# A hybrid decoder block: when block 0's attention is released, and how far apart the two parts of the gates lie

## The chip, the cores and the metric

One core of a Trainium2 chip runs the whole program. The metric is the device time of one execution in microseconds (us), the median of several runs. Engines: TensorE (PE) multiplies, VectorE (DVE), ScalarE (ACT) and GpSimd (POOL) do the elementwise work, SyncE (SP) and ACT issue the loads and stores.

## The reference

One layer, batch 1, 2048 tokens, width 1024, all in float32. The parts that matter here:

```python
h = modulate(rms_norm(x, g_pre_mix), shift_m, scale_m)
q_a, k_a, v_a, q_m, k_m, v_m, o_m, i_m, f_m, g_a, g_m = split(h @ w_in)
y_a = sliding_window_attention(rope(q_a), rope(k_a), v_a, sinks)    # window 128, 8 query heads, 2 kv heads of 64
y_m = sigmoid(o_m) * head_layer_norm(mlstm_chunkwise(silu(conv(q_m, k_m)), v_m, i_m, f_m))
mix = (sigmoid(g_a) * (y_a @ w_branch_attn) + sigmoid(g_m) * (y_m @ w_branch_mlstm)) @ w_out
x = x + gate_m * rms_norm(mix, g_post_mix)
h2 = modulate(rms_norm(x, g_pre_ffn), shift_f, scale_f)
x = x + gate_f * rms_norm((silu(h2 @ w_ffn_gate) * (h2 @ w_ffn_up)) @ w_ffn_down, g_post_ffn)
```

The attention of 128 query tokens is a softmax over the 256 keys of its own and the previous block of 128, with a learned sink per head. The mLSTM needs, per token and head, running sums of log f and a running maximum of the input gate: these come from `i_m` and `f_m`, and are "the gates" below.

## The kernel before, in words

The 2048 tokens are two superblocks (`sb`) of two token blocks `b0` and `b1` of 512. For every superblock PE computes, in this order: the q products of a block (512 columns), its key, value and gate products together (`kv`, 264 columns), and the mLSTM value products (`vm`), for b0 and then for b1; then the pairs (`om`, `qk`, `ga`, `gm`), each of which shares products between the two blocks; then mLSTM, branch projections and outputs. Matmuls are exact to about float32: each operand is split into a high and a low part in fp32r, and `mm3` (L212 is the line in `mm` that issues) multiplies high by high, high by low and low by high. The split of weights is `split`: a cast on ACT, a subtraction on DVE (L264 and L265, L267 and L268 where a load is split in two). Superblock 1 reads split weights of `kv`, `q` and `vm` that superblock 0 stored to DRAM (`w_kv_d`, `w_q_d`, `w_vm_d`, loads at L328 and L333).

**What sets the order.** `superblock` is a generator of `Part`s (some weights with the products that use them) and of small functions that are called where they stand. Beside it run streams: generators that are started with `spawn(gen, delay)` and yield, after each step, the delay until their next step. The delays (`L_...`, in ns) are counted in PE's planned time (`now`, to which each `mm` adds); `tick` issues whatever is due, and `finish` drives streams to their end. Last, the framework's scheduler reorders each engine's instructions by its own estimate of time, so a moved call shifts instructions on all engines around it.

**The streams of this change.** `gates(b)` has three steps. The first does elementwise work on the gates' 32 columns; after `L_GATE` the second transposes them (PE L217 on `gt`), scans them on DVE (L905, L909) and forms maxima (L910 to L918); after `L_SCAN` the third transposes the results (four 68-column transposes, PE L217 on `tm`) and copies them out.

`attention_stream(u)`, u = 0 or 1, does every second of the superblock's eight attention blocks of 128 queries: it loads the queries, keys and values (`at`, L954; written to `at_d` before), and `attention` does 24 score products (12 for block 0 of all), in two halves: after each, ACT copies the scores of the own keys (L985), and DVE puts in those of the window before (L987). Then the maxima (DVE L993 to L996), eight exponentials with their sums (ACT L1002), reciprocals (DVE L1003, L1004) and the division (POOL L1005). After `L_SOFT` PE transposes each half (L217 on `tm`), ACT (L1014) and DVE (L1018) copy the two masks of it, and PE multiplies with the values (16 products); ACT and DVE split the result (L1030, L1035), and ACT stores it. The two streams start `L_ATT2` apart. A stream waits at blocks of b1 until `ready` says that b1's q and kv exist.

`attend(b)` finishes the rotary work on q and k, sets `ready`, starts the two attention streams if b is b0, and starts `gates(b)`. In superblock 0 it is called for b0 behind b0's vm; in superblock 1 behind b0's kv, ahead of vm; for b1 behind a quarter of b1's vm. Scores, transposes and value products use four PSUM banks in turn (`mix`); projections use the others (`acc`), which ACT empties (for vm, L870).

Of the kernel before, what the change touches and what calls it, by code (L numbers as in the profile page):

```python
# [37 lines left out]

L_X, L_HT, L_HS = 16000.0, 1400.0, 1500.0
L_ROPE, L_ROPEK, L_QK, L_ATT2 = 5000.0, 2100.0, 1500.0, 3500.0  # L40
L_GATE, L_SCAN = 1800.0, 5500.0
L_SOFT, L_PT, L_PV = 8000.0, 1300.0, 1000.0
L_ML, L_KW, L_OUT, L_STATE = 3200.0, 2600.0, 1500.0, 1500.0
L_S, L_LN = 1800.0, 5000.0
# [29 lines left out]
def decoder_block(ctx: ExitStack, tc: tile.TileContext, a: dict, out: bass.AP, dbg=None):  # L74
# [49 lines left out]
    def tx(shape, dtype=F32):  # L124
        return tpool.tile(shape, dtype, tag="tx", name=nm("tx"), bufs=9)
# [93 lines left out]
    def spawn(gen, delay=0.0):  # L219
        st = [now[0] + delay, gen, False]  # L220
        streams.append(st)
        return st
# [15 lines left out]
    def finish(sts):  # L238
        for st in sts:
            while not st[2]:  # L240
                now[0] = max(now[0], min(q[0] for q in streams))
                tick()
# [190 lines left out]
    b1 = const.tile([P, 48], F32, name="b1")  # L433
# [130 lines left out]
    def hsums(names):  # L564

        for name in names:
            raw = HR.pop(name)
            lo = hc_part(name, 1)
            nc.sync.dma_start(lo.bitcast(F32), raw)
        yield L_HD  # L570
        for name in names:
            hi, lo = (hc_part(name, i) for i in range(2))
            for k in range(4):
                v = lo[:, k, :].bitcast(F32)
                A.copy(hi[:, k, :], v)
                V.tensor_tensor(lo[:, k, :], v, hi[:, k, :].bitcast(F32), op=ALU.subtract)
                yield L_HS
# [191 lines left out]
    def superblock(sb):  # L769
        b0, b1 = 2 * sb, 2 * sb + 1  # L770
# [8 lines left out]
        def rope(raw, heads, b, t):  # L779
            sin, cos = tables[sb]  # L780
            t += (b % 2) * NT
            W = heads * HD
            raw = raw[:, :W]
            src = raw.rearrange("p (h u f) -> p h u f", u=2, f=32)
            cb = cos[:, t, :].unsqueeze(1).to_broadcast([P, heads * 2, 32])
            sb_ = sin[:, t, :].unsqueeze(1).unsqueeze(1).to_broadcast([P, heads, 2, 32])
            z = tx([P, 512])
            zz = z[:, :W].rearrange("p (h u f) -> p h u f", u=2, f=32)
            rr = raw.rearrange("p (h f) -> p h f", f=32)
            V.tensor_tensor(zz, src[:, :, ::-1, :], sb_, op=ALU.mult)  # L790
            V.tensor_tensor(rr, rr, cb, op=ALU.mult)
            V.tensor_tensor(src[:, :, 0, :], src[:, :, 0, :], zz[:, :, 0, :], op=ALU.subtract)
            V.tensor_tensor(src[:, :, 1, :], src[:, :, 1, :], zz[:, :, 1, :], op=ALU.add)
            return raw, z

        def q_stream(b, t, yz):
            yield L_ROPE
            y, z = yz
            pt = mix_tile()
            for j in range(GQ):  # L800
                transpose(pt[:, j * P:(j + 1) * P], y[:, j * P:(j + 1) * P])
            hi, lo = z.bitcast(F32R), y.bitcast(F32R)
            A.activation(hi, pt, AF.Copy, scale=HD ** -0.5)
            V.scalar_tensor_tensor(lo, pt, HD ** -0.5, hi.bitcast(F32), op0=ALU.mult, op1=ALU.subtract)
            for i, q in enumerate((hi, lo)):
                nc.sync.dma_start(at_d[b * NT + t][:, i * 512:(i + 1) * 512], q.bitcast(F32))
# [50 lines left out]
        def q_kv(b):  # L857
            if b > 1:
                q = token_group(kept_weights("q"), KD, 512, lhs_h(b), evac_q(b), kept=True)
            else:  # L860
                q = token_group(srcs_rows(w_in, KD, C_Q), KD, 512, lhs_h(b), evac_q(b), pair_heads=True, store="q" if b else None)
            if b > 1:
                return q, token_group(kept_weights("kv"), KD, 264, lhs_h(b), evac_kv(b), kept=True)
            raw_kv = Raw(load_kv)
            return q, token_group([(raw_kv, (lambda r, j=j: r[:, j:j + 2, :]), j, 2) for j in range(0, KD, 2)], KD, 264, lhs_h(b), evac_kv(b), store="kv" if b else None)

        def vm(b):
            def evac(t, ps):
                v = tx([P, 512])
                A.copy(v, ps)  # L870
                nc.sync.dma_start(vm_d[b][:, t, :], v)
            if b > 1:
                yield from token_group(kept_weights("vm"), KD, 512, lhs_h(b), evac, kept=True)
            else:
                yield from token_group(srcs_rows(w_in, KD, C_VM), KD, 512, lhs_h(b), evac, store="vm" if b else None)
# [69 lines left out]
        def load_at(n, queue):  # L945
            a_ = at()
            af = a_.bitcast(F32)
            if n == 0:
                queue.dma_start(af[:, :AT_K], at_d[n][:, :AT_K])
                for c0, k in ((AT_K, 2), (AT_V, 1)):  # L950
                    v_, d_ = (z[:, c0:c0 + 2 * k * P].rearrange("p (i u k) -> p i u k", i=k, u=2)[:, :, 1, :] for z in (af, at_d[n]))
                    queue.dma_start(v_, d_)
            else:
                queue.dma_start(af, at_d[n])  # L954
            return a_
# [86 lines left out]
        def attention_stream(u):  # L1042
            a_ = None
            for i in range(u, 2 * NT, 2):
                n = b0 * NT + i
                if a_ is None:
                    while i >= ready[0]:
                        yield 1000.0
                    a_ = load_at(n, nc.sync)
                    yield L_LOAD  # L1050
                    a_ = yield from attention(n, a_, lambda: i + 2 < ready[0])
                else:
                    yield L_LOAD - 1500.0
                    a_ = yield from attention(n, a_, lambda: i + 2 < ready[0])
                done_att[0] += 1
                yield 500.0
# [3 lines left out]
        def attend(b):  # L1060
            finish(R["qk"])
            ready[0] = (b - b0 + 1) * NT
            if b == b0:
                R["att"] = [spawn(attention_stream(0), L_QK), spawn(attention_stream(1), L_QK + L_ATT2)]
            R["gs", b] = [spawn(gates(b), L_QK)]

        def end_attention(n):
# [285 lines left out]
        if sb == 0:  # L1353
            raws, rotated = {}, {}

            def late_q(t):
                yield from q_stream(b0, t, rope(raws[t], HQ, b0, t))

            def q_raw(t, ps):
                raws[t] = tx([P, 512])  # L1360
                A.copy(raws[t], ps)
                if t > 1:
                    R["qk"].append(spawn(late_q(t), L_KV0 + L_LATE * (t - 1)))

            def q_rope(t):
                rotated[t] = rope(raws[t], HQ, b0, t)

            def q_rest(t):
                for _ in q_stream(b0, t, rotated[t]):
                    pass  # L1370

            first.update(kv=kv0, evac=q_raw, rope=q_rope, rest=q_rest)
        else:
            yield start
            yield from q0
            yield from kv0
            yield lambda: attend(b0)
        yield from vm(b0)
        yield lambda: finish([hps[b1]])
        if sb == 0:  # L1380
            yield lambda: attend(b0)
        yield lambda: hps.update(t=spawn(hsums(("T2", "T4"))))
        q1, kv1 = (list(z) for z in q_kv(b1))
        yield from kv1
        yield from q1
        vm1 = list(vm(b1))
        yield from vm1[:len(vm1) // 4]
        yield lambda: attend(b1)
        yield from vm1[len(vm1) // 4:]

        def start_f():
# [809 lines left out]
    def program():  # L2201
        items = [it for sb in range(NSB) for it in superblock(sb)]
        last = max(i for i, it in enumerate(items) if isinstance(it, Part))
        first_block()
        yield from items[:last]
        yield lambda: next(phase2)
        yield from items[last:]
# [47 lines left out]
```

## Time and profile before

| | before |
|---|---|
| median of 3 runs | 2666.65 us (2666.62 to 2668.6) |
| profiled execution | 2664.19 us |
| its span, 36035 instructions | 2662.2 us |
| mean granted PE clock | 0.996 |
| PE busy | 2614.5 us (98%), 12546 products and transposes |
| DVE, ACT, POOL busy | 1935.3, 1281.4, 133.1 us |

A row of the profile names the engine, the line of the kernel, the operation, and output <- input with the names in the program; behind it stand sizes, counts and times. In rows of the timeline the two numbers ahead are start and duration in us, and a bracket shows idle time ahead of the row and what ended it. Products overlap on PE, so a row's duration is longer than the distance to the next.

### The profile page before, as it was taken

How to read it: one execution, taken by the hardware profiler on the slowest of the kernel's cores; microseconds unless marked ns; L12 is line 12 of the kernel's file. 1: busy time of each engine (PE TensorE's matmuls, PEld its weight loads, DVE VectorE, ACT ScalarE, POOL GpSimd, SP SyncE). 2: the span in 40 equal slices, each digit the busy share in tenths (PEclk: the TensorE clock that was granted, in tenths of full speed). 3: DMA queues.
4: the chain of work that ended last, by engine and by line, in shares of the span. 5: the costliest groups of instructions: out<-in, count | busy, mean ns of one | idle time of the engine just before them, and what ended most of it. 6: DMA issues, size and time to landing. Idle time of an engine off the chain costs nothing.

```text
span 2662.2 us, 36035 instructions
## 1 busy us (share of the span) xinstructions
PE 2614.5 (98%) x12546; PEld 2142.4 (80%) x12546; DVE 1935.3 (73%) x3758; ACT 1281.4 (48%) x2531; POOL 133.1 (5%) x181
## 2 busy tenths in 40 slices
PE   8999999999989999999999999999999999999998
PEld 6777788888877788888878888888778888888786
DVE  6878887768675988875877777776776767676466
ACT  6656544545654654454643433345544333333444
POOL 0000001101100000110000000000000000000000
PEclk9999999999999999999999999999999999999999
DMA  7794466897797545597766554547675323234556
GB/s 270 255 327 141 135 194 186 266 327 247 263 311 241 179 135 185 181 301 261 224 235 199 172 174 155 165 136 232 211 241 173 111 99 113 94 111 138 191 204 221
DMA packets 352166, 532.95 MB, mean 200 GB/s; under 512 B 23136, under 2 KB 209628, under 8 KB 345200
## 3 DMA queue, kind: packets, MB, share of 16 engines
q1 hardware_dynamic: 333768, 514.86, 57.8%
q10 hardware_dynamic: 18216, 15.79, 1.9%
q8 instruction: 99, 1.62, 0.2%
q14 instruction: 83, 0.68, 0.1%
HBM read 367.61 MB, written 154.57 MB: 196 GB/s over the span
## 4 chain that ended last, share of the span: by engine, by line
PE 88%; DVE 5%; DMA 4%; ACT 2%; issue 1%; POOL 0%; ACTq 0%; SPq 0%; DVEq 0%; POOLq 0%
PE acc L212 61%; PE mix L212 23%; PE mix L217 2%; DVE hl L1745 1%; PE acc L90 1%; PE mix L90 1%; ACT hl L1744 1%; DMA raw<-as_d 1%; ACT tm L1002 1%; DMA raw<-ws_d 0%; DMA raw<-w_kv_d 0%; DMA big<-in_x_dram 0%; DMA raw<-in_w_ffn_down_dram 0%; DMA at_d<-tx 0%; DMA raw<-in_w_in_dram 0%
## 5 line engine op out<-in xcount | busy, mean ns | idle before, releaser
L212 PE MATMUL acc<-big,hl 128*128 128x512 f32 x3936 | 936.0, 392 | 4.0 <-ACT hl L1744 1.8
L212 PEld LDWEIGHTS acc<-big,hl 128*128 128x128 f32 x3936 | 732.3, 188 | 164.4 <-issue 5.1
L1744 ACT CAST hl<-raw 128x512 fp32r<-128x512 f32 x732 | 439.9, 621 | 491.7 <-PE acc L212 216.3
L1745 DVE TENSOR_TENSOR hl<-raw,hl 128x512 fp32r<-128x512 f32 x732 | 496.6, 695 | 200.7 <-ACT hl L1744 197.1
L212 PE MATMUL acc<-whi,big 128*128 128x512 f32 (+1 forms) x896 | 279.3, 387 | 0.1
L212 PE MATMUL mix<-big,hl 128*128 128x512 f32 x1056 | 263.0, 390 | 1.8 <-ACT hl L1744 1.1
L212 PE MATMUL acc<-hl,hl 128*128 128x512 f32 x1008 | 237.3, 393 | 5.8 <-DVE hl L1745 3.0
L212 PEld LDWEIGHTS mix<-big,hl 128*128 128x128 f32 x1056 | 197.7, 188 | 44.6 <-ACT hl L1744 2.0
L212 PEld LDWEIGHTS acc<-hl,hl 128*128 128x128 f32 x1008 | 187.0, 188 | 51.5 <-DVE hl L1745 8.7
L212 PEld LDWEIGHTS acc<-whi,big 128*128 128x128 f32 x896 | 167.2, 189 | 33.3 <-ACT whi L264 0.4
L212 PE MATMUL mix<-hl,hl 128*128 128x512 f32 x792 | 182.6, 391 | 2.6 <-ACT hl L1744 1.8
L212 PEld LDWEIGHTS mix<-hl,hl 128*128 128x128 f32 x792 | 147.9, 188 | 36.5 <-ACT hl L1744 3.0
L212 PE MATMUL acc<-wlo,big 128*128 128x512 f32 (+1 forms) x448 | 173.4, 388 | 1.1 <-DVE wlo L265 1.1
L212 PE MATMUL acc<-big,whi 128*128 128x512 f32 x512 | 157.4, 393 | 0.0
L268 DVE TENSOR_TENSOR wlo<-raw,whi 128x1024 fp32r<-128x1024 f32 (+1 forms) x76 | 91.2, 1200 | 60.9 <-ACT whi L267 55.7
L267 ACT CAST whi<-raw 128x1024 fp32r<-128x1024 f32 (+1 forms) x76 | 78.3, 1031 | 93.9 <-PE acc L212 87.3
L492 POOL TENSOR_TENSOR rs<-ms,halves 128x1 f32<-128x1 f32 (+1 forms) x56 | 41.0, 739 | 1635.8 <-DVE ms L490 1589.2
L212 PE MATMUL mix<-hcT4h,hl 128*128 128x512 f32 x352 | 115.6, 389 | 0.7 <-ACT hl L1744 0.7
L212 PE MATMUL acc<-hcT2h,hl 128*128 128x512 f32 x352 | 115.5, 389 | 0.0
L212 PEld LDWEIGHTS acc<-big,whi 128*128 128x128 f32 x512 | 95.3, 188 | 19.3
L212 PEld LDWEIGHTS acc<-wlo,big 128*128 128x128 f32 x448 | 85.0, 190 | 18.8 <-DVE wlo L265 1.4
L212 PE MATMUL acc<-big,wlo 128*128 128x512 f32 x256 | 97.5, 392 | 0.0
(379 smaller groups left out, 3640.7 us busy)
## 6 DMA issues: line engine op xcount, KB each, us to landing
as_d<-w SPq DMA_DIRECT2D x154, 256.0 KB, 2.0
raw<-in_w_in_dram SPq DMA_DIRECT2D x36, 1024.0 KB, 5.4
raw<-as_d SPq DMA_DIRECT2D x70, 512.0 KB, 3.8
raw<-in_w_ffn_gate_dram SPq DMA_DIRECT2D x22, 1024.0 KB, 5.6
raw<-in_w_ffn_up_dram SPq DMA_DIRECT2D x22, 1024.0 KB, 6.0
raw<-ws_d SPq DMA_DIRECT2D x40, 512.0 KB, 4.7
tx<-in_w_ada_dram SPq DMA_DIRECT2D x64, 256.0 KB, 5.3
g_d<-tx SPq DMA_DIRECT2D x64, 256.0 KB, 4.5
```

The costliest lines, as they stand in the source:

```text
L90: self.last = tc.keep_in_program_order(f(*p, **k)).ins
L212: T.matmul(o, lhsT=lhsT, rhs=rhs, start=start, stop=stop, skip_group_check=resumed)
L217: T.transpose(o, i, ident[:k, :k])
L267: A.copy(hv, src)
L268: V.tensor_tensor(lv, src, hv.bitcast(F32), op=ALU.subtract)
L492: G.tensor_tensor(r[:, :n], ms[:, :n], nhalf[:, :n], op=ALU.pow)
L1002: A.activation(sc[jj][:, i, :], sc[jj][:, i, :], AF.Exp, bias=nm_[:, c:c + 1], accum_out=sums[:, c:c + 1])
L1744: A.copy(v(hi), src)
L1745: V.tensor_tensor(v(lo), src, v(hi).bitcast(F32), op=ALU.subtract)
```

## The change

`attend(b)` no longer starts the gates; a new `gate(b)` does, with the same delay. For b0, `gate(b0)` stands where `attend(b0)` stood, and `attend(b0)` stands behind the key and value products of b1, ahead of b1's q products in the program. For b1 both are called where `attend(b1)` was. `L_SCAN` goes from 5500 to 20000 ns of PE's planned time.

```diff
-L_GATE, L_SCAN = 1800.0, 5500.0
+L_GATE, L_SCAN = 1800.0, 20000.0
...
             if b == b0:
                 R["att"] = [spawn(attention_stream(0), L_QK), spawn(attention_stream(1), L_QK + L_ATT2)]
+
+        def gate(b):
             R["gs", b] = [spawn(gates(b), L_QK)]
...
             yield from q0
             yield from kv0
-            yield lambda: attend(b0)
+            yield lambda: gate(b0)
         yield from vm(b0)
         yield lambda: finish([hps[b1]])
         if sb == 0:
-            yield lambda: attend(b0)
+            yield lambda: gate(b0)
         yield lambda: hps.update(t=spawn(hsums(("T2", "T4"))))
         q1, kv1 = (list(z) for z in q_kv(b1))
         yield from kv1
+        yield lambda: attend(b0)
         yield from q1
         vm1 = list(vm(b1))
         yield from vm1[:len(vm1) // 4]
-        yield lambda: attend(b1)
+        yield lambda: (attend(b1), gate(b1))
         yield from vm1[len(vm1) // 4:]
```

No instruction is added or taken away, and lines behind the new function stand two or three lower. PE's order is the same up to the second half of b1's kv in superblock 0, differs from there to some way into the pairs, where the attention ends, and differs again over the like stretch of superblock 1.

PE before, superblock 0, at the second half of b1's kv (`whi`, `wlo` are the split weights, `acc` the bank of the kv products, `mix<-at` scores, `tm_1222` the gates' rows):

```order
L212 MATMUL acc_1142<-whi_1193,big_767 128x264
L212 MATMUL acc_1143<-whi_1193,big_767 128x264
L217 MATMUL mix_1339<-ident,tm_1222 128x68 x4
L212 MATMUL mix_1366<-at_1247 128x256 x6
L212 MATMUL mix_1367<-at_1247 128x256 x6
L212 MATMUL mix_1384<-at_1247 128x256 x6
L212 MATMUL acc_1140<-wlo_1194,big_767 128x264
```

PE of the change, the same place:

```order
L212 MATMUL acc_1143<-wlo_1135,big_678 128x264
L212 MATMUL acc_1143<-whi_1134,big_679 128x264
L212 MATMUL acc_1140<-whi_1189,big_767 128x264
L212 MATMUL acc_1141<-whi_1189,big_767 128x264
L212 MATMUL acc_1142<-whi_1189,big_767 128x264
L212 MATMUL acc_1143<-whi_1189,big_767 128x264
L212 MATMUL acc_1140<-wlo_1190,big_767 128x264
```

Scores and gate transposes no longer stand between the products with the high part of the weights and the first one with the low part.

PE of the change, superblock 0, where b1's vm ends and the first pair begins (`at_1667` and `at_1714` are two attention blocks, `tm_1722` and `tm_1723` the two halves of the first one's softmax, `tm_1822` of the second's, `tx` rows of rotary work, `acc_2539` the pair's first bank):

```order
L212 MATMUL mix_1842<-at_1714 128x256
L212 MATMUL mix_1843<-at_1714 128x256
L217 MATMUL mix_1890<-ident,tm_1722 128x128 x4
L217 MATMUL mix_1899<-ident,tx_1792 128x128 x4
L217 MATMUL mix_1911<-ident,tx_1805 128x128 x4
L217 MATMUL mix_1920<-ident,tm_1723 128x128 x4
L212 MATMUL mix_1951<-tm_1895,at_1667 64x256 x2
L212 MATMUL mix_1951<-tm_1897,at_1667 64x256 x2
L217 MATMUL mix_1966<-ident,tx_1880 128x128 x4
L217 MATMUL mix_1978<-ident,tm_1822 128x128 x4
L212 MATMUL mix_1951<-tm_1925,at_1667 64x256 x2
L212 MATMUL acc_2539<-big_382,hl_2127 128x512
```

PE before, at the last scores of an attention block in b1's vm of the same superblock (its softmax is transposed some eighty rows below):

```order
L212 MATMUL acc_1545<-wlo_1842,big_767 128x512
L212 MATMUL mix_1668<-at_1579 128x256 x6
L212 MATMUL acc_1545<-whi_1841,big_768 128x512
L212 MATMUL acc_1546<-whi_1841,big_767 128x512
L212 MATMUL acc_1546<-wlo_1842,big_767 128x512
```

In the changed order the transposes of a block's softmax follow its last scores with two products and the next block's scores between; before, products of vm lay between.

SP's issues in superblock 1 before (`raw<-w_kv_d` are the two loads of b1's key and value weights, `big` parts of h):

```order
L954 DMA at_7481<-at_d_198 128x1792
L954 DMA at_7545<-at_d_199 128x1792
L333 DMA raw_7547<-w_kv_d 128x2112
L569 DMA big_8010<-big_6927 128x2048
L569 DMA big_8012<-big_6529 128x2048
L328 DMA whi_8117<-w_q_d 128x1024
L333 DMA raw_7721<-w_kv_d 128x2112
L328 DMA wlo_8118<-w_q_d 128x1024
```

and of the change:

```order
L333 DMA raw_7543<-w_kv_d 128x2112
L569 DMA big_7646<-big_6927 128x2048
L569 DMA big_7648<-big_6529 128x2048
L328 DMA whi_7719<-w_q_d 128x1024
L328 DMA wlo_7720<-w_q_d 128x1024
L954 DMA at_7877<-at_d_198 128x1792
L333 DMA raw_7572<-w_kv_d 128x2112
L954 DMA at_7896<-at_d_199 128x1792
```

The first load of the weights is now ahead of both attention loads, and the second one behind one of them.

## The prediction

> **What bounds the kernel now.** I read the page's busy times and its chain first, then the table of what TensorE (PE) waits for, then windows, and last the single rows of the windows that stand out. Page parts 1 and 4:
>
> ```profile
> PE 2614.5 (98%) x12546; PEld 2142.4 (80%) x12546; DVE 1935.3 (73%) x3758; ACT 1281.4 (48%) x2531; POOL 133.1 (5%) x181
> PE 88%; DVE 5%; DMA 4%; ACT 2%; issue 1%; POOL 0%; ACTq 0%; SPq 0%; DVEq 0%; POOLq 0%
> ```
>
> PE is busy for 2614.5 of 2662.2 us and holds 88% of the chain, so time can only come from stretches in which PE stands still or runs at a lower granted clock. The edit leaves the number of products at 12546. What PE waits for at the lines that the edit touches (us in total, times, longest):
>
> ```profile
> PE mix L217 <- POOL tm L1005: 6.1, 5, 2.2
> PE acc L212 <- DMA raw<-w_kv_d: 3.0, 1, 3.0
> PE mix L217 <- DVE tm L912: 1.6, 1, 1.6
> PE acc L212 <- DVE wlo L265: 1.1, 1, 1.1
> PE acc L212 <- ACT tx L870: 1.3, 2, 0.8
> ```
>
> Two stretches carry nearly all of this. In the windows the first column is the stretch, the second its length, then busy time per engine, the granted PE clock, the DMA share and GB/s:
>
> ```profile
> 100.00:150.00 50.00, 44.92 (x270) 36.53 (x269) 34.55 (x108) 27.96 (x88) 4.28 (x4) 0.90 0.89 309
> 750.00:800.00 50.00, 43.10 (x269) 35.93 (x268) 36.19 (x118) 26.15 (x81) 4.43 (x4) 0.93 0.94 330
> 850.00:900.00 50.00, 47.99 (x252) 37.12 (x252) 49.13 (x108) 33.81 (x88) 4.28 (x4) 1.00 0.69 239
> 104.00:108.00 4.00, 2.37 (x25) 1.90 (x24) 3.91 (x10) 1.29 (x4) 0.00 (x0) 0.84 1.03 383
> 108.00:112.00 4.00, 4.00 (x25) 3.65 (x24) 3.94 (x12) 1.75 (x4) 0.00 (x0) 0.50 0.99 352
> 112.00:116.00 4.00, 4.00 (x28) 3.87 (x27) 2.69 (x9) 0.00 (x0) 0.00 (x0) 0.81 0.96 319
> 765.00:770.00 5.00, 3.83 (x17) 3.86 (x18) 2.99 (x7) 1.50 (x3) 0.00 (x0) 0.55 1.02 426
> ```
>
> The first (superblock 0) loses 50 - 44.92 = 5.1 us of idle time and 0.10 x 50 = 5.0 us of clock, 10.1 in all; the second (superblock 1) 6.9 + 3.5 = 10.4. The clock fell to 0.50 right behind idle stretches (2.37 busy of 4), so an idle stretch of some us here costs about its length and then half of the next few us. 20.5 us, 0.8%, is all that a perfect repair of these two places could bring.
>
> **Part 1, superblock 0, the second half of block 1's keys and values.** PE's rows there before, with the idle time ahead of a row in brackets, and VectorE's (DVE):
>
> ```profile
> 103.42 1.44 PE L212 MATMUL mix<-at 64*128 64x128 f32 x21
> 107.73 0.69 PE L217 MATMUL mix<-ident,tm 68*128 68x68 f32 x4 [1.63 <-DVE tm L912]
> 121.48 0.66 PE L217 MATMUL mix<-ident,tm 128*128 128x128 f32 x4 [2.23 <-POOL tm L1005]
> 123.86 0.79 PE L212 MATMUL acc<-wlo,big 128*128 128x512 f32 x1 [1.08 <-DVE wlo L265]
> ...
> 101.52 1.35 DVE L905 TENSOR_TENSOR_SCAN tm<-ones,tm 4x128 f32<-4x128 f32 x4
> 102.79 1.25 DVE L909 TENSOR_TENSOR_SCAN tm<-tm,m_last,tm 4x512 f32<-4x512 f32 x1
> 107.17 0.42 DVE L912 TENSOR_SCALAR tm<-tm 4x512 f32<-4x512 f32 x1
> 108.36 0.69 DVE L268 TENSOR_TENSOR wlo<-raw,whi 128x528 fp32r<-128x528 f32 x1
> ```
>
> Two edits meet here. The longer delay L_SCAN puts the four 68-column transposes of the gates some 200 products later: their 1.63 us go, and nobody waits for them soon. The later release takes away the attention scores that filled PE from 103.42 on. What PE has left at 103.42 is four products without the low part of the weights, some 0.5 us; the low part is made by the row at 108.36, which stands on DVE behind the same gate scans and sums as before and ends at 109.05. PE waits 109.05 - 103.9 = 5.1 us. The clock: before, two half-speed stretches followed 1.63 us of waiting; behind 5.1 us I take the 0.50 up to about 113.5, that is 4.4 us of work at half speed, 2.2 lost. The next weights (q of block 1) were late by 1.08 at 123.86 and should be late by about as much again, 1.1 (0 to 3, their buffers come free when stores land). In return the 2.23 us ahead of 121.48 go, since the first softmax then has 10 us or more of products over it. So 5.1 + 2.2 + 1.1 = 8.4 for 10.1: **-1.7 us** (-5.0, if neither clock nor weights cost anything, to +1.4, with 3.4 of clock and 3 of weights).
>
> **Part 2, superblock 0, the start of the pairs: a new wait.** Attention that starts later ends at the same place, so it is packed closer. In the changed order PE issues, at the end of the second mLSTM value products: the last six scores of one attention block (L212, reading `at`), 2 products, all 24 scores of the next block, and at once the transposes of the first block's softmax, 8 rotary transposes, the second half's transposes, the value products, the next block's transposes, and only then the first product of a pair, whose PSUM bank must first be emptied by ScalarE (ACT, L870) behind all of that. Before, every block had 8 us and more of other products between its last score and its transposes. Prices from before:
>
> ```profile
> 118.04 0.40 ACT L1002 ACTIVATE tm<-tm,nmx 128x128 f32<-128x128 f32 x1
> ...
> 120.85 0.38 ACT L1002 ACTIVATE tm<-tm,nmx 128x128 f32<-128x128 f32 x1
> L1005 POOL TENSOR_TENSOR tm<-tm,sums 128x512 f32<-128x512 f32 x16 | 16.8, 1050 | 190.3 <-DVE sums L1004 148.6 <-PE acc L212 32.5 <-ACT tm L1002 6.3
> L985 ACT COPY tm<-mix 128x256 f32<-128x256 f32 x32 | 10.3, 377 | 12.1 <-PE mix L212 12.0
> L1744 ACT CAST hl<-raw 128x512 fp32r<-128x512 f32 x40 | 24.4, 620 | 16.0 <-PE acc L212 13.4 <-DVE raw L1838 2.2 <-ACT tm L1014 0.2
> L1014 ACT COPY tm<-mix 128x512 f32<-128x512 f32 x16 | 8.9, 586 | 0.4 <-ACT tm L1030 0.4
> L993 DVE TENSOR_REDUCE mx<-tm 128x4 f32<-128x512 f32 x16 | 10.8, 677 | 0.0
> 759.74 1.79 PE L212 MATMUL mix<-at 64*128 64x256 f32 x24 [0.85 <-DMA at<-at_d]
> ```
>
> A softmax's eight exponentials and the sink's take ACT from 118.04 to 121.2, 3.2 us. Count from the first block's last score. Copy 0.4, two casts of the pair's operands that stand ahead (1.2), their DVE halves and a maximum (0.7 each): the bias is there at 3.4, half of the exponentials at 5.1, POOL's 1.05 behind their sums gives 6.5. PE has 2 products and the 24 scores (1.79), 2.3 us: 4.2 idle. The second half is ready at 8.0, about when PE has done the rotary transposes. The value products need DVE's second use of the transposes, which stands behind ACT's four copies of the next block (1.5), one copy (0.6), and DVE's masks and two maxima: about 10.2, 1.7 idle. The next block's exponentials start at 11.2; its first POOL product is there at 14.4, 3.0 idle; ACT is free for L870 at about 15.1, and the pair's first product can go at 15.7. PE's own work up to there is about 6.1, so 9.6 us are lost, and half clock behind it takes 1.4 more: **+11 us** (6 to 16). The lower end is ACT's bare sum in that order, 0.4 + 1.2 + 3.2 + 1.5 + 0.6 + 1.2 + 3.2 + 1.2 = 12.5, less 6.1; the upper end has 1.7 more for the four L870 copies, 2 more clock, and a DVE that is late at the start. [...]
>
> **Part 3, later in superblock 0.** Of L1005's 6.1 us, 2.2 are at 121.48 and 1.85 in superblock 1 (below); the other 2.0 and the 1.3 of L870 stand later in superblock 0, at blocks that the new order has already done: **-2.3 us** (-3.3 to 0).
>
> **Part 4, superblock 1.** PE's rows, and SyncE's issues:
>
> ```profile
> 766.17 4.30 PE L212 MATMUL acc<-raw,big 128*128 128x264 f32 x18 [3.05 <-DMA raw<-w_kv_d]
> 785.64 0.65 PE L212 MATMUL mix<-tm,at 128*64 128x256 f32 x4 [0.24 <-ACT tm L1014]
> 786.67 1.08 PE L212 MATMUL mix<-tm,at 128*64 128x256 f32 x8 [0.38 <-DVE tm L1018]
> 788.28 0.65 PE L212 MATMUL mix<-tm,at 128*64 128x256 f32 x4 [0.53 <-DVE tm L1018]
> 790.79 0.66 PE L217 MATMUL mix<-ident,tm 128*128 128x128 f32 x4 [1.85 <-POOL tm L1005]
> 753.27 1.15 SPq L954 DMA_DIRECT2D at<-at_d  x2
> 754.48 0.43 SPq L333 DMA_DIRECT2D raw<-w_kv_d  x1
> 755.00 1.39 SPq L569 DMA_DIRECT2D big<-big  x2
> 757.11 0.39 SPq L333 DMA_DIRECT2D raw<-w_kv_d  x1
> ```
>
> PE waited 3.05 us for key and value weights that were issued behind two attention loads (0.9 MB each), with the DMA engines full (share 1.02, 426 GB/s at 765 to 770). In the changed order the first weights' load goes ahead of both; it is issued at about 753.3, 1.1 MB, and is there by 760. PE wants it at 766.17 - 3.05 - 0.85 - 1.79 = 760.5: no wait. The second load goes behind two `big` loads (2.1 MB), w_q (1.05) and one attention load (0.9): with its own 1.1 that is 5.15 MB from 758 at 0.40 MB/us (between the windows' 330 and 426 GB/s), 770.9. The first half's 48 products take 0.12 each (18 take 4.3 us in the row at 766.17, at about half clock), so PE wants it at about 767: 3.9 us idle, 1.7 of clock, and the next w_q load some 1.8 us late behind it, 7.4 in all. The 3.0 us of the last four PE rows go, since block 1's q products (12 us and more) now lie between scores and transposes. 7.4 for 10.4: **-3.0 us** (-8.4, if only the w_q wait is left, to +1).
>
> **The sum.** -1.7 + 11 - 2.3 - 3.0 = +4.0 us on the profiled execution's 2664.19 us (2662.2 of span and 2.0 around it): 2668.2. The median of the runs lies 2.5 above that execution, so 2670.7.
>
> **The rivals.**
> - *The bunch at the pairs is covered* (faster). For it: before, a softmax with too little over it cost PE 2.23 and 1.85 us, not 11; if the two blocks cost no more than one such wait together, part 2 is +1, and the sum is -1.7 + 1 - 2.3 - 3.0 = -6.0: 2660.6. Against it: both rows had one block to wait for; here two follow each other on ACT, and a bank that ACT must empty stands behind.
> - *Superblock 1's pairs run into a full DVE* (slower). From 850 to 900 DVE is busy for 49.13 of 50 us and PE already loses 2.0. Attention moved behind the keys brings a further block's masks, maxima, sums, transposed copies and residual there: 4 x 0.44 + 2 x 0.68 + 2 x 0.68 + 0.69 + 0.4 = 5.6 us of DVE by the sort of rows above, against 0.9 us of room. It decides from the point at which one block more lies in that window. Then 4.0 + (5.6 - 0.9) = +8.7: 2675.4. Against it: the gates' scans leave DVE's earlier stretch in exchange.
> - *The change moves stalls about* and the terms cancel: 0, 2666.7. This is the middle of the forecast's own range; it is also what is seen if the bunch costs ACT's bare 6 us (-1).
>
> **How the numbers follow.** This kernel tells a difference from no change at about 0.2%, 5.3 us. The forecast with the cancelling case (2661.3 to 2672.0) gets 0.39, the covered bunch 0.24, the full DVE or a bunch at its upper end 0.37. The four terms' ends are far apart and not of one cause; the range 2658 to 2678 reaches past the covered bunch's 2660.6 and the slower case's 2675.4 and leaves 0.1 out at each side.
>
> **What would show it.** Part 1: one wait of PE of about 5 us on `wlo` L268 near 104, none on L912, none of 2.2 on L1005 near 121. Part 2: near 160 to 190 us PE waits on L1005, L1018, L1014 and L870 of about 10 us in all, with a clock under 1. Part 4: the wait on w_kv_d near 767 instead of 763, of 4 us, and none on `at`. The prediction is wrong if PE's loss at the start of superblock 0's pairs is under 4 us (then faster), or if a window of superblock 1 behind 850 loses over 4 us more than before (then slower).

## The result, and the profile after

| | before | changed |
|---|---|---|
| median, 6 runs each | 2667.62 us (2663.59 to 2670.24) | 2679.22 us (2675.9 to 2682.33) |
| ratio, 95% interval | | 1.0046 (1.0035 to 1.0057) |
| profiled execution | 2664.19 us | 2678.47 us |
| its span, mean granted clock | 2662.2 us, 0.996 | 2676.2 us, 0.993 |

The change makes the kernel slower, by 11.6 us on the medians. The forecast was no difference that can be told, at 2670.7, with a range to 2678. Page part 1 of the changed kernel:

```profile
PE 2624.9 (98%) x12546; PEld 2149.5 (80%) x12546; DVE 1937.4 (72%) x3758; ACT 1282.5 (48%) x2531; POOL 135.4 (5%) x181
```

DVE, ACT and POOL work as long as before. PE shows 10 us more of busy time for the same 12546 products, most of which is half clock (up to the last ten us of the span the clock is at 0.50 for 30.7 us, before for 17.1); the other 4 us of the span are idle. The windows of both kernels do not lie over the same work, since the changed one is late, so the places are told apart in another way: PE issues 12546 products in both, in the same order except in two stretches. The start of PE's product number n in one profile, less that in the other, says how much was lost up to there:

| stretch of PE's products | before starts it at | changed kernel's loss in it | forecast |
|---|---|---|---|
| 0 to 500, order the same | 0 | +2.9 | 0 |
| 500 to 1710, superblock 0 (parts 1 to 3) | 92.2 | +7.2 | +7.0 |
| 1710 to 3590, order the same | 323.6 | 0.0 | 0 |
| 3590 to 5000, superblock 1 (part 4) | 711.2 | +4.4 | -3.0 |
| 5000 to the end, order the same | 969.4 | -0.8 | 0 |

PE's waits in the changed kernel, of the whole execution, those that have to do with the edit:

```profile
PE acc L212 <- DVE wlo L268: 4.7, 1, 4.7
PE mix L217 <- DVE tm L987: 4.5, 1, 4.5
PE mix L212 <- DVE tm L922: 2.8, 1, 2.8
PE mix L217 <- POOL tm L1005: 1.6, 3, 0.7
PE mix L217 <- ACT gt L845: 1.2, 1, 1.2
PE mix L217 <- DVE tx L793: 1.0, 1, 1.0
PE acc L212 <- DMA raw<-w_kv_d: 0.3, 1, 0.3
```

The waits that the edit was to touch are gone or smaller (L912, `w_kv_d` 3.0 to 0.3, L1005 6.1 to 1.6), and new ones of some 14 us in all (L268, L987, L922, L845, L793) stand in their place.

**Superblock 0.** PE's rows, the chain of ACT behind the first block's last scores, and POOL:

```profile
107.36 0.74 PE L212 MATMUL acc<-whi,big 128*128 128x264 f32 x4 [0.96 <-ACT whi L267]
112.78 0.59 PE L212 MATMUL acc<-wlo,big 128*128 128x264 f32 x1 [4.67 <-DVE wlo L268]
...
177.20 0.97 PE L212 MATMUL mix<-at 64*128 64x256 f32 x6
179.54 1.69 PE L212 MATMUL mix<-at 64*128 64x256 f32 x24 [0.72 <-DMA at<-at_d]
185.78 1.09 PE L217 MATMUL mix<-ident,tm 128*128 128x128 f32 x4 [4.55 <-DVE tm L987]
192.61 0.66 PE L217 MATMUL mix<-ident,tm 128*128 128x128 f32 x4 [0.69 <-POOL tm L1005]
193.78 3.04 PE L212 MATMUL acc<-big,hl 128*128 128x512 f32 x12
...
181.61 0.40 ACT L1002 ACTIVATE tm<-tm,nmx 128x128 f32<-128x128 f32 x1 [1.84 <-DVE nmx L995]
185.44 1.04 POOL L1005 TENSOR_TENSOR tm<-tm,sums 128x512 f32<-128x512 f32 x1 [0.46 <-ACT tm L985]
191.52 1.04 POOL L1005 TENSOR_TENSOR tm<-tm,sums 128x512 f32<-128x512 f32 x1 [5.04 <-DVE sums L1004]
```

The first block's last scores end at about 178.2. Its exponentials begin 3.4 us later and its transposes go at 185.8, 7.6 us later; the first product of a pair goes at 193.78, 15.6 us later. POOL's row at 183.94, not shown, has the first half of the softmax ready at 184.98, 6.8 us behind the scores; the wait of 4.55 us is named L987, DVE's copy of the next block's scores, which stands behind the exponentials. A bank that these scores hold would explain the last 0.8 us; that was not tried. In window terms the stretch from 150 to 200 had 49.19 us of PE at a clock of 1.00 before, and has 44.04 at 0.93:

```profile
150.00:200.00 50.00, 44.04 (x240) 32.90 (x240) 32.46 (x73) 30.82 (x93) 6.25 (x6) 0.93 0.77 263
```

**Superblock 1.** PE's rows and windows, 10.2 us late against before:

```profile
779.71 0.40 PE L212 MATMUL mix<-tm,ones 4*128 4x32 f32 x2 [2.75 <-DVE tm L922]
780.38 7.66 PE L212 MATMUL acc<-raw,big 128*128 128x264 f32 x48 [0.27 <-DMA raw<-w_kv_d]
789.48 0.30 PE L217 MATMUL mix<-ident,tx 128*128 128x128 f32 x1 [1.24 <-ACT gt L845]
790.75 0.30 PE L217 MATMUL mix<-ident,tx 128*128 128x128 f32 x1 [0.97 <-DVE tx L793]
791.63 0.30 PE L217 MATMUL mix<-ident,tx 128*128 128x128 f32 x1 [0.58 <-DVE sp L886]
791.86 3.39 PE L212 MATMUL mix<-at 64*128 64x256 f32 x24
795.18 5.19 PE L212 MATMUL acc<-raw,big 128*128 128x512 f32 x14
...
896.37 0.73 PE L212 MATMUL acc<-big,hl 128*128 128x512 f32 x2 [1.87 <-ACT hl L1747]
```

```profile
775.00:780.00 5.00, 2.25 (x20) 2.04 (x18) 4.60 (x10) 2.28 (x3) 0.00 (x0) 1.00 1.02 430
780.00:785.00 5.00, 4.73 (x28) 4.62 (x28) 0.87 (x9) 0.24 (x1) 0.00 (x0) 0.68 1.03 336
790.00:795.00 5.00, 3.67 (x26) 3.37 (x26) 3.89 (x22) 3.13 (x9) 0.00 (x0) 0.70 1.08 372
795.00:800.00 5.00, 5.00 (x16) 3.82 (x15) 2.55 (x9) 4.41 (x17) 0.31 (x1) 0.61 0.78 262
```

The second load of `w_kv_d` comes just behind the last gate row that PE waits for: both end near 780. Behind the 48 products with it stand the rotary transposes of b1's new keys, four single ones. The first goes at once; each of the other three waits for elementwise work on keys just made, with no product between. Before, they were not there: DVE ended that work at 789.8, and the transposes came 42 us later, among another block's value products, without a wait. The first of them:

```profile
831.45 0.33 PE L217 MATMUL mix<-ident,tx 128*128 128x128 f32 x1
```

They stand right behind kv in the kernels below whose release in superblock 1 is moved (e2, e4, e12, and two of the four in e7), and at the old place in the others. `attend` begins by driving all rotary work under way to its end, and at its new place that takes in these keys. It may not be the whole reason, since e7 calls it before they are made; what puts them there was not tried by itself.

2.75 + 0.27 + 1.24 + 0.97 + 0.58 = 5.8 us are waits. Then there is clock: 48 products take 7.66 us, where 48 at 0.122, the distance of such products before, take 5.9; 24 scores 3.39 for 1.79 before; 14 products of 512 columns 5.19 for about 3.2 (such products followed each other at 0.227 before). That is 5.4 us more, an estimate. 11.2 us stand for the 10.4 that this stretch lost before.

### The profile page after: what moved, and what is told of

Same layout as the page of the kernel before. It is cut to its first block, busy times and chain, and to the rows that moved or that the text cites. A ratio compares the mean times of both kernels' runs of the same rounds, so it can differ in the third digit from the quotient of the medians.

```text
span 2676.2 us, 36050 instructions
## 1 busy us (share of the span) xinstructions
PE 2624.9 (98%) x12546; PEld 2149.5 (80%) x12546; DVE 1937.4 (72%) x3758; ACT 1282.5 (48%) x2531; POOL 135.4 (5%) x181
## 4 chain that ended last, share of the span: by engine, by line
PE 83%; DVE 4%; DMA 2%; ACT 2%; issue 1%; POOL 0%; SPq 0%; DVEq 0%; POOLq 0%; ACTq 0%
PE acc L212 59%; PE mix L212 22%; PE mix L217 2%; DVE hl L1748 1%; DMA raw<-as_d 1%; ACT hl L1747 1%; DMA raw<-ws_d 0%; DMA raw<-w_kv_d 0%; ACT tm L1002 0%; DMA at_d<-tx 0%; DMA raw<-in_w_ffn_down_dram 0%; DVE tm L987 0%; DVE big L1748 0%; DVE w L2058 0%; DMA raw<-in_w_ffn_gate_dram 0%
## 5 line engine op out<-in xcount | busy, mean ns | idle before, releaser
L268 DVE TENSOR_TENSOR wlo<-raw,whi 128x1024 fp32r<-128x1024 f32 (+1 forms) x76 | 90.8, 1194 | 62.6 <-ACT whi L267 54.6
L267 ACT CAST whi<-raw 128x1024 fp32r<-128x1024 f32 (+1 forms) x76 | 78.4, 1031 | 104.8 <-PE acc L212 91.9
```

What stands on the lines that cost most here:

```text
L267: A.copy(hv, src)
L268: V.tensor_tensor(lv, src, hv.bitcast(F32), op=ALU.subtract)
```

## The experiments

Losses in the two stretches are against the profile of before, as in the table above. Ratios are against the kernel before, measured again beside each group of runs, with 95% intervals.

| run | what is moved | ratio | superblock 0 | superblock 1 |
|---|---|---|---|---|
| the change | both, delay 20000 | 1.0046 (1.0035 to 1.0057) | +7.2 | +4.4 |
| e1_scan | only the delay | 1.0000 (0.9991 to 1.0008) | +2.7 | -3.3 |
| e2_move | only the move | 1.0080 (1.0067 to 1.0093) | +9.2 | +5.1 |
| e3_sb0 | the change in superblock 0, delay in both | 1.0034 (1.0021 to 1.0046) | +8.0 | -1.6 |
| e4_sb1 | the change in superblock 1, delay in both | 1.0035 (1.0021 to 1.0048) | +3.2 | +5.7 |
| e5_spread | e3_sb0, streams 9000 apart | 0.9995 (0.9986 to 1.0004) | +1.7 | -2.7 |
| e6_delay1 | only the delay, in superblock 1 | 0.9997 (0.9988 to 1.0006) | +1.4 | -0.9 |
| e7_midkv | e4_sb1, released half a load earlier | 1.0049 (1.0035 to 1.0063) | +2.8 | +3.5 |
| e8_bunch | e6_delay1, streams 9000 apart | 1.0019 (1.0010 to 1.0028) | +4.1 | -2.7 |
| e9_late | e5_spread, gates behind kv in superblock 0 | 0.9993 (0.9984 to 1.0001) | +0.5 | -1.5 |
| e10_later | e9_late, gates behind q | 1.0010 (1.0002 to 1.0019) | +6.5 | -2.6 |
| e11_gates1 | e9_late, gates behind kv in both | 1.0032 (1.0019 to 1.0045) | -0.3 | +8.1 |
| e12_gates_sb1 | e4_sb1, gates behind kv in superblock 1 | 1.0027 (1.0016 to 1.0039) | +1.0 | +4.5 |

e6_delay1 has before's order on every engine until superblock 1: its +1.4 in superblock 0 is what one profile against another leaves uncertain, and differences of 1 to 2 us below are no more than that. In e9_late to e12_gates_sb1 the gates of block 0 are formed, in the superblock named, after block 1's products have overwritten their columns (`gt` is one buffer), so the mLSTM's decays are computed from other numbers; instructions and sizes are the same.

**e1_scan: only the longer delay.**

```diff
-L_GATE, L_SCAN = 1800.0, 5500.0
+L_GATE, L_SCAN = 1800.0, 20000.0
```

> Only the longer delay between the two parts of the gates (L_SCAN 20000); attention is released where it was. Theory A (the moved attention costs the time, place by place: +7.2 us between product 500 and 1710 in superblock 0 and +4.4 between 3590 and 5000 in superblock 1, while the 2.9 us ahead of product 500 are the clock's chance): PE's 1.63 us wait on L912 in superblock 0 and some of the half clock behind it go, so 1 to 5 us faster than before. Rival B (gates that end later make the wait, through what stands behind them): slower by 5 us or more. Rival C (the 2.9 us ahead of product 500 belong to the edit): they are there too.

No difference. In superblock 0 the wait on L912 went and others came, on the same DVE chain and behind it:

```profile
112.92 0.39 PE L212 MATMUL acc<-wlo,big 128*128 128x264 f32 x1 [1.34 <-DVE wlo L268]
118.76 0.39 PE L212 MATMUL acc<-wlo,big 128*128 128x264 f32 x1 [2.66 <-DVE wlo L268]
127.23 0.79 PE L212 MATMUL acc<-whi,big 128*128 128x512 f32 x1 [3.74 <-ACT tx L840]
```

So the gain that theory A gave the delay there was wrong, and so was rival B's loss. That the 2.9 us ahead of product 500 are seen here too (3.0) is what rival C said; e6_delay1 (2.0, with before's order on all engines) and e8_bunch (0.2) settle it: they are chance (see the last section).

**e2_move: only the move** (the change with `L_SCAN` at 5500).

> Only the move of block 0's attention behind block 1's keys and values, with the old delay (L_SCAN 5500). Theory A: slower than before by about as much as the whole change, +8 to +15 us, with the bunch at the start of superblock 0's pairs (4.5 us on PE ahead of the softmax's transposes). Rival B: within 4 us of before, since the gates are where they were.

20 us slower, more than the whole change and more than theory A's 15. The two superblocks account for 14.3; some 4 to 5 of the rest are lost far away, behind product 7000, where the FFN starts. ACT's first copy there waits for a store of x:

```profile
1405.67 0.58 ACT L1888 COPY w<-acc 128x512 f32<-128x512 f32 x1 [5.73 <-DMA x<-tm]
```

Before, that copy came without a wait. The same 4 us are in e7_midkv and e8_bunch and in no other kernel. Which buffer the tile gets seems to depend on how the streams were interleaved; this was not tried by itself.

**e3_sb0 and e4_sb1: the change in one superblock.** The release of b0 stays where it was in the other one (`if sb == 0` or `if sb == 1` around the new call, and the old call beside `gate(b0)`); the delay is 20000 in both.

> The whole change in superblock 0; in superblock 1 attention is released where it was, with the longer delay of the gates. Theory A: superblock 0 keeps its +7 us, superblock 1 loses none or gains a little: +4 to +8 us against before. A rival (superblock 1 is the one that costs; superblock 0's 7 us are clock chance): within 3 us of before.

> The whole change in superblock 1; in superblock 0 attention is released where it was, with the longer delay of the gates. Theory A: superblock 0 gains 1 to 5 us by the delay, superblock 1 loses 4: -1 to +4 us against before. The rival (superblock 1 is the one that costs): +8 us or more.

Each superblock costs about the same, 0.34% and 0.35% of the whole. Several of the kernels have one order on PE in a stretch, so the move can be set against the delay alone by means: in superblock 0, (7.2 + 8.0) / 2 with it, (2.7 + 3.2 + 2.8 + 1.0) / 4 = 2.4 without (e1_scan, e4_sb1, e7_midkv, e12_gates_sb1), 5.2 us for the move; in superblock 1, 4.4 and 5.7 with it, (-3.3 - 1.6 - 0.9) / 3 = -1.9 without (e1_scan, e3_sb0, e6_delay1), some 7 us. Of these 7, half clock is the larger part: superblock 1's traces have 13.7 us (the change) and 10.2 us (e4_sb1) at a clock of 0.50, and 3.4 in each of the three without the move, which is 3.4 to 5.1 us of time. Both runs cost over 8 us on the medians, just above what theory A gave e3_sb0 and twice its most for e4_sb1: superblock 0 had no gain from the delay, and superblock 1 lost 5.7 where 4 were put. e4_sb1 alone would fit its rival; e3_sb0 rules it out.

**e5_spread: the bunch taken away.**

```diff
-L_ROPE, L_ROPEK, L_QK, L_ATT2 = 5000.0, 2100.0, 1500.0, 3500.0
+L_ROPE, L_ROPEK, L_QK, L_ATT2 = 5000.0, 2100.0, 1500.0, 9000.0
```

> e3_sb0 (the whole change in superblock 0 only) with the second attention stream started 9000 instead of 3500 ns behind the first (L_ATT2), in both superblocks. In PE's order every attention block of superblock 0 then has 9 us or more of products between its last score and its transposes, where e3_sb0 has 2.3 and 3.0 for two of them at the start of the pairs. Theory A (this bunch costs what part 2 says, 9 to 11 us with its clock): the 4 to 5 us wait at the start of the pairs is gone and superblock 0 (products 500 to 1710) takes 4 to 9 us less than in e3_sb0. Rival (moved softmaxes cost by DVE's load wherever they are): within 2 us of e3_sb0.

Superblock 0 falls from +8.0 to +1.7, as theory A has it, and the whole kernel from 1.0034 to 0.9995. PE's rows with a wait from 160 to 200 us, e3_sb0 first, then e5_spread:

```profile
180.01 1.69 PE L212 MATMUL mix<-at 64*128 64x256 f32 x24 [0.40 <-DMA at<-at_d]
186.84 1.09 PE L217 MATMUL mix<-ident,tm 128*128 128x128 f32 x4 [5.13 <-DVE tm L987]
193.67 0.66 PE L217 MATMUL mix<-ident,tm 128*128 128x128 f32 x4 [1.06 <-POOL tm L1005]
```

```profile
178.36 0.65 PE L212 MATMUL mix<-tm,at 128*64 128x256 f32 x4 [0.87 <-DVE tm L1018]
181.02 3.02 PE L212 MATMUL acc<-big,hl 128*128 128x512 f32 x12 [1.42 <-ACT tx L870]
```

The same softmaxes are moved behind the same products; with 9 us over each of them they cost nothing that one profile can tell (+1.7 against the +1.4 of e6_delay1). The cost of the move in superblock 0 is the bunch; the 4.7 us on L268 are still there in e5_spread.

**e6_delay1: the delay in superblock 1 alone** (`yield (20000.0 if sb else L_SCAN)`).

> The kernel before with the longer delay of the gates in superblock 1 alone (20000 there, 5500 in superblock 0). From e1_scan's profile, whose superblock 1 took 3 us less than before's and whose superblock 0 took 3 us more: 1.5 to 3.5 us faster than before, if these two numbers are the edit's; no difference if they are the clock's chance.

No difference that can be told (-0.9 us in superblock 1, where e1_scan with the same order on PE had -3.3 and e3_sb0 -1.6).

**e7_midkv: attention released between the two loads of kv** (the call stands behind `kv1[:len(kv1) // 2]`).

> e4_sb1 (the whole change in superblock 1 only) with block 0's attention released after the first half of block 1's keys and values instead of after both. PE's order then has scores and kv products between the rotary transposes of the new keys. Theory A (in superblock 1 the loss is cover: the waits on L922 and on the rotary transposes' inputs, L793 and L845, about 6 us, and the clock behind them): these waits go for the larger part, and superblock 1 takes 3 to 8 us less than in e4_sb1. Rival (the order of the loads on SyncE costs it): the wait on w_kv_d comes back with 3 us or more and superblock 1 takes as long as in e4_sb1.

Superblock 1 takes 2.2 us less than in e4_sb1, under the 3 to 8 expected: waits on L922 (2.6) and L793 (2.6) stay, L870 adds 4.2, and `w_kv_d` waits 0.5. The rival did not hold either, and 2.2 us are hardly more than two profiles differ by. The total holds the 4 us at the FFN's start.

**e8_bunch: a bunch without the move** (e6_delay1 with `L_ATT2` at 9000).

> e6_delay1 with the second attention stream 9000 instead of 3500 ns behind the first. Here the longer distance makes a bunch: one attention block of superblock 0 has 2.0 us of products between its last score and its transposes. Theory A: PE waits there for 4 us or more, superblock 0 takes 3 to 7 us longer than in e6_delay1. Rival: no difference.

The same distance that took the bunch away in e5_spread makes one here, and superblock 0 takes 4.1 - 1.4 = 2.7 us more than in e6_delay1, with a wait of 3.0 us on L1005. Both are a little under what was expected (3 to 7, and 4 or more). The ratio of 1.0019 holds the 4 us at the FFN's start as well.

**e9_late and e10_later: the gates out of the way of the kv weights.**

```diff
-        if sb == 0:
-            yield lambda: gate(b0)
         yield lambda: hps.update(t=spawn(hsums(("T2", "T4"))))
         q1, kv1 = (list(z) for z in q_kv(b1))
         yield from kv1
         if sb == 0:
-            yield lambda: attend(b0)
+            yield lambda: (attend(b0), gate(b0))
```

> e5_spread with the gates of block 0, too, released behind block 1's keys and values in superblock 0. DVE then makes the low part of the last kv weights ahead of the gates' scans. Theory A (part 1: these scans, with nothing left over them, are the 4.7 us wait on L268 and the clock behind it): the wait goes, and superblock 0 (products 500 to 1710) takes 4 to 8 us less than in e5_spread; the kernel is 3 to 8 us faster than before. Rival (PE then waits as long for the next weights or for the gates): within 2 us of e5_spread.

> As e9_late, with the gates of block 0 one step later still in superblock 0, behind block 1's q products. Theory A: as e9_late, within 2 us of it. Rival: as there.

e9_late is within 2 us of e5_spread in superblock 0: the rival. The wait on L268 went, and PE waited 6.6 us for the cast ahead of it, whose buffer a store still held:

```profile
PE acc L212 <- ACT whi L267: 6.6, 1, 6.6
...
113.96 0.63 ACT L267 CAST whi<-raw 128x528 fp32r<-128x528 f32 x1 [8.67 <-DMA w_kv_d<-whi]
109.93 0.43 SPq L374 DMA_DIRECT2D w_kv_d<-whi  x1
105.32 4.57 SPq L806 DMA_DIRECT2D at_d<-tx  x4
```

SyncE issues that store at 109.9, behind four stores of rotated queries that hold its queue from 105.3 to 109.9. So DVE's scans were the last of two waits at this place, not the only one; whether products over it would do was not tried. e10_later missed: superblock 0 takes 6 us more than in e9_late, with 3.2 us on L870 at the pairs and the clock at 0.50 for 6.8 us from 179.8, where e9_late has none.

**e11_gates1 and e12_gates_sb1: the gates behind kv in superblock 1**, with attention where it was and with attention moved.

> As e9_late, with the gates of block 0 behind block 1's keys and values in superblock 1 as well; attention stays where it was there. SyncE's first load of w_kv_d then goes ahead of both attention loads, the second behind both. Theory A (cover and the order of loads): the 3 us wait on w_kv_d moves to the second load and shrinks to 0 to 2 us, since scores lie over it; superblock 1 takes 0 to 3 us less than in e9_late. Rival: the wait is as long, no difference.

> e4_sb1 with the gates of block 0 also behind block 1's keys and values in superblock 1. No scan or transpose of the gates and no attention load is ahead of the second load of w_kv_d or its products. Theory A (superblock 1 loses because the waits on DVE and on the load have nothing over them, and end together): the 2.9 us on L922 go, 1 to 2.5 us on w_kv_d take their place, the rotary transposes still wait 2 to 3.5 us; superblock 1 takes 1 to 4 us less than in e4_sb1. Rival (the gates' place is what costs): superblock 1 is as in the kernel before or faster.

e11_gates1 missed by far: the wait on `w_kv_d` shrank to 0.6 us as expected, but PE then waited 5.7 us for attention loads (3.2 the longest), 3.1 on L870 and 3.4 on L1014. e12_gates_sb1 came out near theory A. PE's waits there, 730 to 985 us, and e4_sb1's below:

```profile
PE mix L217 <- DVE sp L888: 3.2, 1, 3.2
PE acc L212 <- DMA raw<-w_kv_d: 2.3, 1, 2.3
PE mix L217 <- DVE tx L793: 1.0, 2, 0.6
```

```profile
PE mix L217 <- DVE tx L793: 3.1, 3, 1.6
PE mix L212 <- DVE tm L922: 2.9, 1, 2.9
```

The 2.9 us on L922 went and 2.3 on `w_kv_d` came. The four transposes wait 4.7 us, more than the 2 to 3.5 expected: 3.2 of it, on L888, is the last one's wait for the gates' first step, which stands behind kv now. Superblock 1 takes 1.2 us less, no more than one profile leaves uncertain. Taking one wait of this stretch away, even with a load less ahead of the weights, leaves the next one.

No version beats the kernel before: e5_spread and e9_late lie within their intervals of it.

## Why the prediction was wrong, point by point

- **Part 1 held.** A wait of 5.1 us on L268 was forecast near 104; it was 4.67, behind 0.96 on the cast of L267, near 107 to 113, and the clock fell to 0.50, for 6.83 us from 109.4. The 1.1 us for the next weights did not come. By the windows from 100 to 150 the stretch lost 9.2 us for 10.1, so -0.9 for the -1.7 forecast. What the part did not see is a second wait hidden under it, for the store of the split weights (e9_late).
- **Part 2 had the chain right and its split wrong.** Exponentials 3.4 us behind the last score (measured 3.4), POOL's first product of the next block at 14.4 (14.4), first pair product at 15.7 (15.6); so 9.5 us are lost up to there, as forecast. But the part had 9.6 of them as idle time and 1.4 of half clock behind; measured are 0.72 + 4.55 + 0.69 = 6.0 idle, the rest half clock within the stretch (0.50 from 184.5 to 191.3), and none behind it. The waits on L1018, L1014 and L870 did not come, and the main one was named L987.
- **Parts 1 to 3 together** gave +7.0, and products 500 to 1710 lost 7.2. That the two agree so well is partly luck: part 2 was some 1.5 too high, part 1 some 0.8 and part 3 some 0.6 too favourable (PE's idle time from 150 to 300 us outside the bunch was 2.7 before and 1.0 after, 1.7 less for the forecast 2.3). e5_spread and e8_bunch show that the bunch is the cause.
- **POOL's price in part 2 held**: 1.05 us for a product was forecast, and the four of this chain took 1.04 each. Elsewhere in the changed kernel one subtraction on DVE that starts within POOL's product ends 0.55 us behind it, after 1.15 us. The rows of that line that meet no work of POOL take 0.65 to 0.70, and some that start within it do so too (0.68 at 415.91); what held this one was not tried. The two rows:

```profile
229.06 1.04 POOL L1005 TENSOR_TENSOR tm<-tm,sums 128x512 f32<-128x512 f32 x1 [0.50 <-ACT tx L1226]
229.50 1.15 DVE L1748 TENSOR_TENSOR hl<-raw,hl 128x512 fp32r<-128x512 f32 x1 [0.61 <-ACT hl L1747]
```

- **Part 4 failed.** It gave -3.0 us, 7.4 for 10.4; measured is +4.4. The arrival of the second load was right (770.9, measured 780.4 less the 10.2 by which the kernel was late), and its wait was 2.75 + 0.27 = 3.0 for the 3.9 forecast, under the name of L922, which ends at the same time. The forecast 1.8 us for w_q did not appear. Wrong were two terms. The clock was put at 1.7 and took 5.4: idle time came in two portions, before and behind the 48 products, and half clock followed each (0.50 for 3.41 us from 781.8 and for 6.83 us from 792.0). And one term was put at nothing: the rotary transposes of b1's new keys, which the changed order has right behind kv, waited 2.8 us; before, they stood 42 us behind their inputs. The part asked what the moved scores had waited for, and not what comes to stand in their place; part 1 had put that question to superblock 0. These terms make the stretch 11.2 for 7.4, 3.8 of the 7.4 us by which the part was wrong. Up to 1.7 more is half clock for 3.4 us at the start of the pairs (898 to 901 us), behind a wait of 1.87; idle time as such was 2.0 us in that window before, too. Where the remaining 2 us were lost stays open, and no run removed the transposes' wait or the half clock in superblock 1, so that this part's account rests on the rows alone.
- **The rivals.** "Covered" fell in superblock 0 by the rows above. "Full DVE" named the right sign and nearly the right time (2675.4) for a wrong place, which is luck: DVE from 850 to 900 is busy for 41.65 us (42.52 from 860 to 910, the same work 10 us later), less than the 49.13 before, and PE is idle there for 2.1 us as before; most of what was lost was lost ahead of it.
- **The base.** The profiled execution of before is 2664.19 us; six runs of it have a median of 2667.62. 2.9 us of the difference of the two profiles lie ahead of the edit's first effect on PE's products, and belong to the execution, not to the change. The forecast's margin of 0.2%, 5.3 us, would have been passed by the two superblocks' 11.6 alone.

## What to carry to other kernels

Before a block of work is moved, ask of the place that it leaves what each product behind it waits for, and how long PE has something else to do there. Ask also what else the moved call does (this one ends all rotary work under way), and look in the new order for products that have come to stand right behind their inputs; here four did that had been 42 us behind them. In this kernel two waits (an elementwise chain and a DMA) ended close together at each of the two places, so that removing the one that the profile names showed the other. Where work is released late and must end by the same time, look in the new order for the two shortest distances between a block's last product and the first that needs its elementwise result: adding up the elementwise chain from there to the next product that is not attention's gave 15.7 us for the 15.6 measured. Where idle time comes in separate portions, ask of each what it costs in clock: in superblock 1 of the changed kernel 3.0 and 2.8 us of it were each followed by a stretch at 0.50 (3.41 and 6.83 us), where the forecast had one for the place.

## What the runs showed that was not expected

Executions with the same instructions in the same order lose different amounts to the clock at the same place: before and e6_delay1 have a clock of 1.00 and 0.86 in the windows below. Ahead of product 500 PE stands still for 1.7 to 1.8 us in 5 near 50 us in each of these kernels. The windows from 55 to 60, of before, of the changed kernel, of e6_delay1 (before's order on all engines up to superblock 1), and of e8_bunch:

```profile
55.00:60.00 5.00, 5.00 (x34) 4.51 (x32) 1.90 (x4) 3.28 (x6) 0.00 (x0) 1.00 0.64 208
```

```profile
55.00:60.00 5.00, 5.00 (x21) 4.07 (x21) 1.80 (x3) 0.52 (x2) 0.00 (x0) 0.68 0.53 164
```

```profile
55.00:60.00 5.00, 5.00 (x24) 4.09 (x24) 1.62 (x3) 1.29 (x3) 0.00 (x0) 0.86 0.58 188
```

```profile
55.00:60.00 5.00, 5.00 (x33) 4.48 (x32) 1.92 (x4) 3.12 (x6) 0.00 (x0) 1.00 0.63 208
```

The clock is 1.00 in two and 0.68 and 0.86 in the others, and up to product 500 the thirteen other profiles are behind that of before by 0.2 to 3.2 us. In the traces of before and of the changed kernel half clock comes, between 50 us and the last ten, in nine stretches: one of 3.41 us and two of 6.83 in before, three of each in the changed kernel. One of 3.41 us at a clock of 0.50 costs up to 1.7 us, an estimate from these two numbers. The changed kernel has one from 54.8 us on, behind 1.8 us of idle time, and before has none there behind 1.7; why nearly the same idle time is followed by half clock in one execution and not in another, no run shows. A loss of 2 to 3 us that a single profile shows can be chance (e6_delay1 is 2.0 us behind before at product 500, with before's order on all engines), and a forecast made against one profiled execution carries it.
